# Low halves of twelve weight tiles through ScalarE and an adding DMA, S5 halves moved by ScalarE, and a new order: a one-core Hymba layer on Trainium2

## Chip, core and metric

One NeuronCore of one Trainium2 chip runs the whole layer. The metric is the device time of one execution in microseconds (us); lower is better. The names of the engines are those of the profile: PE (TensorE matmul), PEld (its weight load), DVE (VectorE), ACT (ScalarE), POOL (GpSimd), SP (SyncE, which here only issues DMAs).

## What is computed

Everything is float32, for 1024 positions and a model width of 1024. Cut to what matters here:

```python
z   = (LN of x) @ w_in        # split into S5 input 512 | S5 gate 512 | q-latent 256 |
                              # kv-latent 128 | rotary key 64 | MLA gate 512
# S5: bu = b @ u ; h[t] = a * h[t-1] + k * bu[t]  (complex, 32 groups x 64 states)
#     y = Re(c h) + d u ; gelu ; * sigmoid(y @ w_glu + b_glu) ; * silu(S5 gate)
# MLA: 4 heads, low-rank q and kv, shared rotary key, causal softmax over 128-query blocks
s  = einsum(q, k) * scale ; p = softmax(where(causal, s, -inf)) ; o = p @ v   # * silu(MLA gate)
u  = alpha * x + concat(S5, MLA) @ w_out
out = LayerNorm(u + sigmoid(u @ w_g) * (p_emb @ w_p))
```

## The kernel before

TensorE multiplies in the type fp32r, which holds fewer bits than float32. So every operand is split in two by `split(hi, lo, src)`: hi is a cast of src to fp32r, lo = src - hi. A product is three matmuls (`mm3`: hi*hi, lo*hi, hi*lo). In the profile hi and lo are two tiles, for instance `wh` and `wl` for a tile of the input weights (128 x 1024 elements, loaded as `wr`), or `wth` and `wtl` for the weights of the latents (128 x 896, loaded as `wtr`). The cast runs on ACT or DVE, the subtraction on DVE or POOL.

The input projection is cut into twelve weight tiles m (`w_load(m)`, `w_split(m)`): m = 0 to 3 give the S5 input (`xs`), 4 to 7 the S5 gate (`gs`), 8 to 11 the MLA gate (`gm`). Each tile makes two results `z` (512 columns of positions) of 24 matmuls each: eight slices of the contraction times three products. Four more tiles (`wt_split(k)`) make the latents (`lat`, result `zl`).

The S5 branch works on four blocks b of eight channel groups: `mats` builds the blocks' matrices on DVE (products of powers and parameters in `mo` and `mt`, split into `bbh` and `bbl` for the input side, `vvh` and `vvl` for the output side; TensorE transposes and multiplies them into `wt`, from which `wth`, `wtl`, `kt` come); `usplit` splits the input (`suu`); `state` multiplies (`w`, two halves q, each the sum of an even and an odd part of a PSUM tile), rotates (`rt`), scans over positions and puts the result into `hh`, then splits it into `hu`; `out` multiplies again (`y`). Half of the partitions of the S5 tiles hold real parts and half imaginary parts, and for the scan they have to change places: in `state`, a half-partition `add` of 64 x 256 writes from partitions 64..127 to 0..63 and the reverse (`re`, `im`), and half-partition subtractions and additions of 64 x 508 do it again for `hh`.

Attention (`scores`, `probs_t`, `pv`, `uv_out`) follows for 16 pairs of head and query-block pair (list `ATTEND`). DVE adds the mask and takes the row maximum `mx` in one instruction, a second one multiplies `mx` by -SCALE, and ACT takes the exponential. Then come `glu`, the output projection (`op`), the gate (`g`) and the final norm.

What sets the order: no instruction is issued where it is written. All are recorded (so all have one line in the profile, that of the recording helper: L449 before, L456 after), and `Plan.issue` places them by a list scheduler with a cost for each instruction and a priority. The priority is the place in the program, which for the side streams is set by lists of numbers (`MAIN`, `S5`, `LAT`, `GLU`, with `SHIFT`, `AHEAD`, `S5_LATE`). The planner also picks DVE or POOL for the operations that may go to either (`VG`); `NOT_G` lists tiles whose operations may not go to POOL. The result is a fixed order for each engine, and semaphores do the rest. Tiles of 128 x 1024 come from a pool of 40 buffers.

Of the kernel before, what the change touches and what calls it, by code (L numbers as in the profile page):

```python
# [34 lines left out]
P = 128  # L35
# [4 lines left out]
G = 32  # L40
# [12 lines left out]
def _cw_parts(c, bits, n):  # L53
# [11 lines left out]
PI_LO = float(np.nextafter(np.float32(math.pi), np.float32(0)))  # L65

MAIN = [
    ("w_load", 11), ("w_split", 9), ("w_load", 10), ("gm", 0, 0), ("w_split", 11), ("gm", 0, 1), ("gm", 1, 0),
    ("w_split", 10), ("wt_load",), ("gm", 1, 1), ("gm", 2, 0), ("wt_split", 1), ("gm", 2, 1), ("wt_split", 3),
    ("wt_split", 0), ("gm", 3, 0), ("gm", 3, 1), ("wt_split", 2), ("lat", 2), ("lat", 0), ("lat", 3), ("lat", 4),  # L70
    ("w_load", 4), ("w_load", 7), ("w_split", 4), ("w_load", 5), ("lat", 5), ("lat", 6), ("lat", 1), ("w_split", 5),
    ("lat", 7), ("w_load", 6), ("gs", 1, 0), ("gs", 0, 0), ("w_split", 7), ("w_split", 6), ("gs", 1, 1), ("gs", 0, 1),
    ("gs", 2, 0), ("gs", 2, 1), ("gs", 3, 0), ("gs", 3, 1),
]


S5 = [
    (0, "in", 0), (0, "mats", 0), (0, "mats", 0), (0, "usplit", 0), (0, "mats", 1), (0, "state", 0), (1, "mats", 1),
    (1, "in", 1), (2, "out", 0), (3, "mats", 1), (4, "mats", 0), (5, "usplit", 1), (6, "in", 2), (6, "mats", 2),
    (7, "state", 1), (7, "out", 1), (7, "mats", 2), (10, "mats", 2), (11, "phase", 1), (11, "usplit", 2),  # L80
    (11, "in", 3), (11, "state", 2), (13, "mats", 3), (14, "out", 2), (16, "mats", 3), (21, "mats", 3),
    (23, "usplit", 3), (26, "state", 3), (30, "out", 3),
]
# [25 lines left out]
class _Engine:
# [12 lines left out]
class Plan:  # L122
# [122 lines left out]
    @staticmethod  # L245
    def cost(eng, method, out, ins, kw):
        n = 1
        for d in out.shape[1:]:
            n *= d
        for a in ins:  # L250
            m = 1
            for d in a.shape[1:]:
                m *= d
            n = max(n, m) if method in ("bn_stats", "tensor_reduce", "activation") else n
        k = n / 1000.0
        ptr = sum(0.06 for x in ("scalar", "scalar1", "scalar2") if hasattr(kw.get(x), "ap"))
# [20 lines left out]
        if eng == "G":  # L277
            if kw.get("op") == ALU.pow:
                return 0.35 + 210 * k
            if method == "memset":  # L280
                return 0.03 + 0.88 * k
            return 0.25 + 0.82 * k if method == "tensor_scalar" else 0.16 + 2.14 * k
        return 0.06

    @staticmethod
    def shares(eng, method, out, ins):

        if eng == "G":
            return bool(ins)
# [26 lines left out]
    def issue(self):  # L316
# [69 lines left out]
        while len(order) < n:  # L386
# [66 lines left out]
def trunk(ctx, tc, I, out):  # L453
# [472 lines left out]
    def scores(h, qb):  # L926
# [723 lines left out]
```

## Time and profile before

| | before |
|---|---|
| median of 3 runs (lowest to highest) | 581.96 us (581.68 to 582.23) |
| the profiled execution: its own time, its span | 582.14 us, 580.4 us |
| TensorE clock granted, mean | 0.989 of full speed |
| busy: PE / PEld | 558.5 us (96%) / 475.5 us (82%) |
| busy: DVE / ACT / POOL | 455.3 us (78%) / 275.8 us (48%) / 90.1 us (16%) |
| moved by DMA | 76.67 MB, mean 132 GB/s |

The span is what the profiler sees of the program; 1.74 us of the profiled execution's time lies around it. Matmuls are pipelined: a matmul of 512 columns is shown with 0.39 us, but the next one starts about 0.23 us later, so "PE busy" says that matmuls follow each other, and the spacing of their starts says at what rate. The program has these stages: LayerNorm, transposes and the first projections (to about 56 us), the rest of the input projections with S5 beside it (to about 265 us), attention with the rest of S5 and the GLU (to about 398 us), output projection and gate (to 572 us), and a tail.

### The profile page before, as it was taken

To read this page: it belongs to the slowest core of one execution; us is meant where nothing else is said; L and a number is where in the kernel's file an instruction comes from. 1 tells how busy PE (TensorE), PEld (TensorE's weight loads), DVE (VectorE), ACT (ScalarE), POOL (GpSimd) and SP (SyncE) were. 2 spreads that over 40 slices of the span, in tenths; PEclk is the share of its full clock that TensorE was granted. 3 is DMA by queue.
4 is the path that set the end of the run, shared out by engine and by line. 5 is a ranking of instruction groups with operands and counts; after the bars stand their busy time and mean duration, and the time that the engine had idled before them with its cause. 6 is when DMAs were issued, how large, how long until landed. Compare 5 with 4: busy or idle time off the path is not lost.

```text
span 580.4 us, 8272 instructions
## 1 busy us (share of the span) xinstructions
PE 558.5 (96%) x2934; PEld 475.5 (82%) x2934; DVE 455.3 (78%) x973; ACT 275.8 (48%) x516; POOL 90.1 (16%) x100
## 2 busy tenths in 40 slices
PE   8998979999999999999999999999999999999994
PEld 5776868778888988888889999888888888888884
DVE  5989998899999988875998989876345337577666
ACT  6776324627176555445767887765111114123221
POOL 0100000302111153421622222202000001000000
PEclk9999989999999999999999999999999999999997
DMA  7897541533105222200113232509553567934301
GB/s 281 318 353 260 175 144 53 178 100 119 67 2 187 72 67 102 73 38 37 37 37 110 73 109 78 178 0 362 128 127 78 107 155 252 335 109 164 109 37 72
DMA packets 71865, 76.67 MB, mean 132 GB/s; under 512 B 37952, under 2 KB 52992, under 8 KB 71824
## 3 DMA queue, kind: packets, MB, share of 16 engines
q1 hardware_dynamic: 71824, 76.14, 40.3%
q8 instruction: 23, 0.38, 0.3%
q14 instruction: 18, 0.15, 0.1%
HBM read 50.47 MB, written 25.66 MB: 131 GB/s over the span
## 4 chain that ended last, share of the span: by engine, by line
PE 72%; DVE 18%; ACT 3%; DMA 3%; issue 2%; SPq 1%; POOL 0%; DVEq 0%; POOLq 0%
PE g L449 15%; PE op L449 15%; PE z L449 12%; PE s L449 6%; PE o L449 5%; PE zl L449 4%; PE glu L449 4%; PE y L449 2%; PE pt L449 2%; PE qn L449 2%; DVE bn L449 2%; DMA d_pp<-ppo 1%; DVE rt L449 1%; PE uv L449 1%; DVE p L449 1%
## 5 line engine op out<-in xcount | busy, mean ns | idle before, releaser
L449 PE MATMUL z<-xh,wh 128*128 128x512 f32 x192 | 76.4, 398 | 1.0 <-DVE xt L449 1.0
L449 PE MATMUL z<-xl,wh 128*128 128x512 f32 x192 | 76.5, 398 | 0.0
L449 PE MATMUL z<-xh,wl 128*128 128x512 f32 x192 | 76.0, 398 | 0.0
L449 PE MATMUL g<-wpl,uh 128*128 128x512 f32 (+1 forms) x136 | 51.2, 377 | 0.0
L449 PE MATMUL g<-wph,ul 128*128 128x512 f32 (+1 forms) x136 | 51.2, 376 | 0.0
L449 PE MATMUL g<-wph,uh 128*128 128x512 f32 (+1 forms) x136 | 51.2, 376 | 0.0
L449 PEld LDWEIGHTS z<-xh,wh 128*128 128x128 f32 x192 | 36.6, 191 | 8.5 <-DVE xt L449 1.2
L449 PEld LDWEIGHTS z<-xh,wl 128*128 128x128 f32 x192 | 36.7, 191 | 7.2 <-DVE wl L449 0.5
L449 PEld LDWEIGHTS z<-xl,wh 128*128 128x128 f32 x192 | 36.7, 191 | 6.8
L449 DVE SCALAR_TENSOR_TENSOR xr<-xr,op 128x512 f32<-128x512 f32 x16 | 11.0, 686 | 37.8 <-PE op L449 37.8
L449 ACT CAST uh<-xr 128x512 fp32r<-128x512 f32 x16 | 9.9, 621 | 62.3 <-DVE xr L449 49.0
L449 PEld LDWEIGHTS g<-wph,uh 128*128 128x128 f32 x136 | 25.6, 188 | 4.8
L449 PEld LDWEIGHTS g<-wpl,uh 128*128 128x128 f32 x136 | 25.6, 188 | 4.8
L449 PEld LDWEIGHTS g<-wph,ul 128*128 128x128 f32 x136 | 25.6, 188 | 4.6
L449 DVE CUSTOM_DVE_ANT_0 p<-s,mask 128x128 f32<-128x128 f32 (+7 forms) x32 | 23.7, 750 | 4.7 <-PE s L449 4.6
L449 ACT ACTIVATE sgg<-g 128x512 f32<-128x512 f32 (+1 forms) x17 | 9.6, 565 | 36.9 <-PE g L449 36.9
L449 DVE TENSOR_TENSOR ptl<-pt,pth 128x512 fp32r<-128x512 f32 (+3 forms) x48 | 25.6, 552 | 1.4 <-ACT pth L449 0.7
L449 ACT ACTIVATE p<-p,mx 128x128 f32<-128x128 f32 (+7 forms) x32 | 24.6, 771 | 3.6 <-DVE mx L449 3.4
L449 POOL TENSOR_TENSOR yml<-ymt,ymh 128x256 fp32r<-128x256 f32 x16 | 16.6, 1041 | 62.8 <-ACT ymh L449 56.7
L449 PE MATMUL op<-ysh,woh 128*128 128x512 f32 x64 | 24.9, 389 | 0.0
L449 PE MATMUL op<-ysh,wol 128*128 128x512 f32 x64 | 24.9, 389 | 0.0
L449 PE MATMUL op<-ysl,woh 128*128 128x512 f32 x64 | 24.9, 389 | 0.0
(372 smaller groups left out, 1642.4 us busy)
## 6 DMA issues: line engine op xcount, KB each, us to landing
wr<-in_w_fm SPq DMA_DIRECT2D x12, 512.0 KB, 6.1
x<-in_x SPq DMA_DIRECT2D x8, 512.0 KB, 8.9
d_pp<-ppo SPq DMA_DIRECT2D x8, 512.0 KB, 5.9
d_xln<-xt SPq DMA_DIRECT2D x16, 256.0 KB, 6.3
wor<-in_w_out SPq DMA_DIRECT2D x8, 512.0 KB, 5.1
xr<-d_xln SPq DMA_DIRECT2D x8, 512.0 KB, 6.1
d_ut<-ut SPq DMA_DIRECT2D x64, 64.0 KB, 1.9
utok<-d_ut SPq DMA_DIRECT2D x16, 256.0 KB, 4.5
```

Source lines behind the costliest of these rows:

```text
L449: getattr(self.real[ran[i]], method)(*ops[i]["args"], **kw)
```

## The change

It has four parts.

1. Twelve of the sixteen splits of the projection weights (m = 4 to 11, and the four latent tiles) get a new way, `split_dma`: hi is a cast on ACT, lo is written by ACT as -hi, and then a DMA that POOL issues reads the weights from DRAM a second time and adds them onto lo in place.
2. In the softmax the DVE instruction multiplies the masked score by -SCALE itself and takes the minimum, and the exponential takes -1 for its scale. The separate multiplication of `mx` (32 instructions) is gone.
3. In `state`, the sum of the two PSUM parts is one full DVE addition of 128 x 512 and four ACT copies move the halves; for `hh`, two full DVE operations and four ACT copies take the place of four half-partition DVE operations.
4. All lists of the order are new, `S5_LATE` goes from 50 to 260, and `NOT_G` has 19 names instead of 6.

```diff
+    def split_dma(hi, lo, src, dram):
+        cpy(A, hi, src)
+        act(lo, f(hi), AF.Copy, scale=-1.0)
+        Gp.dma_start(out=lo, in_=dram, accum_op=ALU.add)
...
+BY_DMA = range(4, 12)
-        split(h, l, r)                                  # w_split(m)
+        if m in BY_DMA:
+            split_dma(h, l, r, I["w_fm"][m])
+        else:
+            split(h, l, r)
...
-        split(h, l, wt[k])                              # wt_split(k)
+        split_dma(h, l, wt[k], I["w_tm"][k])
...
-            out=so, in0=si, in1=mk, scale=1.0, scalar=3.0 * MASK, op0=ALU.add, op1=ALU.max, accum_out=mx,
+            out=so, in0=si, in1=mk, scale=-SCALE, scalar=-3.0 * MASK, op0=ALU.add, op1=ALU.min, accum_out=mx,
-        V.tensor_scalar_mul(mx, mx, -SCALE)
-        act(p[:, :n], p[:, :n], AF.Exp, scale=SCALE, bias=mx, accum=sm)
+        act(p[:, :n], p[:, :n], AF.Exp, scale=-1.0, bias=mx, accum=sm)
...
             cpy(A, t, ps[:, :, 1])                      # s5_state, for each q
+            add(t, ps[:, :, 0], t)
             for par in range(2):
                 for c, dst in enumerate((re, im)):
-                    src = slice(64 * c, 64 * c + 64)
-                    add(dst[64 * par : 64 * par + 64, 2 * q : 2 * q + 2], ps[src, par::2, 0], t[src, par::2])
+                    cpy(A, dst[64 * par : 64 * par + 64, 2 * q : 2 * q + 2], t[64 * c : 64 * c + 64, par::2])
...
-        n1 = NCH - 1
+        sub(x1, x1, x2)
+        add(x3, x3, x4)
         for par in range(2):
-            r = slice(64 * par, 64 * par + 64)
-            sub(hh[0:64, par::2, 1:], x1[r, :, :n1], x2[r, :, :n1])
-            add(hh[64:P, par::2, 1:], x3[r, :, :n1], x4[r, :, :n1])
+            for c, x in enumerate((x1, x3)):
+                cpy(A, hh[64 * c : 64 * c + 64, par::2, 1:], x[64 * par : 64 * par + 64, :, : NCH - 1])
...
-S5_LATE = 50
-NOT_G = ["bbl", "kd", "mo", "pl", "uql", "vvl"]
+S5_LATE = 260
+NOT_G = ["bbl", "kb", "kd", "p", "ppo", "ppr", "qd", "re", "suu", "tl", "uql", "vvl", "wol", "wpl", "wqrl", "wtl",
+         "wuvl", "xl", "yTl"]
-SHIFT = [(S5, -3920), (LAT, -1380), (GLU, -1400)]
+SHIFT = [(S5, -2680), (LAT, -630), (GLU, -1890)]
```

Counted by engine, with a row for each instruction in the program, DVE has 32 `mx`, 7 `wl` and 2 `wtl` fewer, takes back from POOL the eight `qd`, the eleven scalings of `p` and seven of `kb`, and exchanges 32 half-partition operations of `re` and `im` for 8 full ones, 16 of `hh` for 8. ACT has 8 `wl`, 4 `wtl`, 16 `hh`, 16 `re` and 16 `im` more, and 13 table loads instead of 11. POOL has 12 DMAs. The matmuls are the same.

Where the order moves, at three places.

DVE, before, at the first block of S5 matrices (b = 0). The numbers behind names count tiles in the order of the program; `mo_318` is block 0's input matrix, `mo_351` block 0's output matrix, `ph`, `ec` and `es` are the S5 phases:

```order
L449 TENSOR_TENSOR ph_311<-ec_309,w2c_300 128x8x16
L449 TENSOR_TENSOR ph_312<-es_310,w2s_301 128x8x16
L449 TENSOR_TENSOR mo_318<-pr_248,X_273 128x1024
L449 TENSOR_TENSOR ec_309<-ph_311,ph_312 128x8x16
L449 TENSOR_TENSOR mt_319<-pi_249,Y_274 128x1024
L449 TENSOR_TENSOR ph_311<-ec_309,w2s_301 128x8x16
L449 TENSOR_TENSOR ph_312<-es_310,w2c_300 128x8x16
L449 TENSOR_TENSOR ph_313<-ec_309,w2c_303 128x8x32
L449 TENSOR_TENSOR es_310<-ph_311,ph_312 128x8x16
L449 TENSOR_TENSOR mo_318<-mo_318,mt_319 128x1024
```

And now, where `mo_347` is the input matrix of block 1 and `mo_352` the output matrix of block 0:

```order
L456 TENSOR_TENSOR mo_347<-pr_248,X_273 128x1024
L456 TENSOR_TENSOR mt_348<-pi_249,Y_274 128x1024
L456 TENSOR_TENSOR w2c_306<-w2c_306,w2t_308 128x16
L456 TENSOR_TENSOR mo_347<-mo_347,mt_348 128x1024
L456 TENSOR_TENSOR ph_311<-ec_309,w2c_300 128x8x16
L456 TENSOR_TENSOR ph_312<-es_310,w2s_301 128x8x16
L456 TENSOR_TENSOR mo_318<-pr_248,X_273 128x1024
L456 TENSOR_TENSOR ec_309<-ph_311,ph_312 128x8x16
L456 TENSOR_TENSOR mt_319<-pi_249,Y_274 128x1024
L456 TENSOR_TENSOR bbl_350<-mo_347,bbh_349 128x1024
L456 TENSOR_TENSOR mo_352<-pr_248,CX_277 128x1024
L456 TENSOR_TENSOR mt_353<-pi_249,CY_278 128x1024
```

The addition `mo_318<-mo_318,mt_319` follows six rows later, behind that of `mo_352`. Block 0's input matrix now comes behind those of block 1's input and most of block 0's output. PE, before, at the first use of that matrix (`wt<-ic,bbh`), inside the tile `z_327`, the last of the S5 input:

```order
L449 MATMUL z_327<-xh_150,wh_217 128x512
L449 MATMUL z_327<-xl_151,wh_217 128x512
L449 MATMUL z_327<-xh_150,wl_218 128x512
L449 MATMUL z_327<-xh_154,wh_217 128x512
L449 MATMUL wt_346<-ic_280,bbh_320 128x160 x3
L449 MATMUL wt_347<-ic_280,bbh_320 128x160 x3
```

And now, inside `z_337`, the first tile of the MLA gate, whose weights are the first of the new kind:

```order
L456 MATMUL z_337<-xh_170,wh_325 128x512
L456 MATMUL z_337<-xl_171,wh_325 128x512
L456 MATMUL wt_342<-ic_280,bbh_320 128x160 x3
L456 MATMUL wt_343<-ic_280,bbh_320 128x160 x3
L456 MATMUL z_337<-xh_170,wl_326 128x512
```

The use stands behind four matmuls of `z_327` before, behind all 24 of it and 17 of `z_337` now: 37 matmuls of 512 columns later. ACT, now, at the second weight tile of the new kind (`wh_367` is its hi, `wl_368` its lo):

```order
L456 CAST wh_367<-wr_323 128x1024
L456 COPY kt_341<-wt_344 128x64
L456 CAST wtl_340<-wt_344 128x256
L456 COPY kt_341<-wt_344 128x64
L456 COPY ic_280<-cxh_279 128x8x32
L456 ACTIVATE wl_368<-wh_367 128x1024
```

Between the cast and the negative copy stand four small instructions; in the order before, neither the copy nor a DMA stands there, and DVE subtracts. POOL, now, with the DMAs that add the weights onto lo:

```order
L456 DMA wl_326<-in_w_fm 128x1024
L456 DMA wl_368<-in_w_fm 128x1024
L456 MEMSET zk_335 112x512
L456 DMA wl_371<-in_w_fm 128x1024
L456 TENSOR_TENSOR kt_362<-kt_362,kb_366 128x8x16
```

And PE, now, where that lo is used for the first time:

```order
L456 MATMUL z_395<-xh_150,wh_367 128x512
L456 MATMUL z_395<-xl_151,wh_367 128x512
L456 MATMUL z_395<-xh_150,wl_368 128x512
L456 MATMUL z_395<-xh_154,wh_367 128x512
L456 MATMUL w_381<-suu_359,wth_339 128x256
```

Two matmuls of that tile stand ahead of the one that reads the new lo, and the POOL queue holds the second DMA, a memset and the third DMA ahead of a product for the S5 kernel (`kt`). The second half of the `w` matmuls of `state` for block 0 stands two rows behind it.

More of the change, by code (lines that the diff above doesn't have):

```diff
@@ L67 @@
 MAIN = [
[L68 to L72, printed above, removed]
+    ("w_load", 11), ("gm", 0, 0), ("w_split", 9), ("w_load", 10), ("w_split", 10), ("wt_load",), ("gm", 0, 1),
+    ("w_split", 11), ("gm", 1, 0), ("gm", 2, 0), ("gm", 2, 1), ("wt_split", 0), ("wt_split", 1), ("wt_split", 2),
+    ("gm", 1, 1), ("wt_split", 3), ("lat", 0), ("gm", 3, 0), ("w_load", 4), ("gm", 3, 1), ("lat", 6), ("w_load", 5),
+    ("lat", 4), ("lat", 7), ("lat", 2), ("w_load", 6), ("w_split", 5), ("lat", 5), ("w_split", 6), ("gs", 1, 0),
+    ("lat", 3), ("w_load", 7), ("w_split", 4), ("gs", 0, 0), ("gs", 1, 1), ("lat", 1), ("gs", 0, 1), ("w_split", 7),
     ("gs", 2, 0), ("gs", 2, 1), ("gs", 3, 0), ("gs", 3, 1),
@@ L77 @@
 S5 = [
[L78 to L82, printed above, removed]
+    (0, "mats", 0), (0, "in", 0), (0, "mats", 1), (0, "mats", 0), (0, "usplit", 0), (0, "mats", 1), (1, "state", 0),
@@ L83 @@
+    (3, "mats", 0), (3, "in", 1), (4, "mats", 1), (4, "usplit", 1), (6, "out", 0), (6, "mats", 2), (8, "in", 2),
+    (8, "state", 1), (8, "out", 1), (9, "mats", 2), (10, "mats", 2), (11, "usplit", 2), (12, "phase", 1),
+    (13, "state", 2), (13, "out", 2), (14, "in", 3), (14, "mats", 3), (20, "mats", 3), (23, "mats", 3),
+    (25, "usplit", 3), (26, "state", 3), (30, "out", 3),
 ]
 LAT = [
-    (16, "lat_alloc"), (17, "lat_norm", 1), (17, "lat_transpose", 1), (17, "lat_norm", 0), (19, "fold"),
@@ L86 @@
-    (20, "lat_transpose", 0), (20, "q_rope", 1), (20, "q_rope", 0), (21, "mask"), (23, "q_nope", 0, 0),
-    (23, "q_rope_t", 0), (23, "q_rope_t", 1), (24, "q_nope", 0, 1), (27, "q_nope", 1, 0), (27, "q_nope", 2, 0),
-    (27, "q_nope", 1, 1), (27, "q_nope", 2, 1), (27, "q_nope", 3, 0), (27, "q_nope", 3, 1),
+    (10, "lat_alloc"), (17, "lat_norm", 1), (19, "lat_norm", 0), (20, "mask"), (20, "lat_transpose", 1), (20, "fold"),
+    (20, "lat_transpose", 0), (20, "q_rope", 0), (22, "q_nope", 2, 0), (22, "q_rope", 1), (23, "q_rope_t", 0),
@@ L89 @@
+    (23, "q_nope", 0, 0), (23, "q_nope", 0, 1), (24, "q_rope_t", 1), (27, "q_nope", 1, 0), (27, "q_nope", 1, 1),
+    (30, "q_nope", 2, 1), (30, "q_nope", 3, 0), (30, "q_nope", 3, 1),
 ]
 GLU = [
-    (30, "glu_y", 2), (31, "glu_w"), (33, "glu_y", 0), (34, "glu_gs", 1), (35, "glu_gs", 2), (36, "glu_y", 1),
-    (37, "glu_yg", 2), (38, "glu_yg", 1), (38, "glu_gs", 3), (39, "glu_y", 3), (39, "glu", 1, 0), (39, "wo_load", 1),
-    (39, "glu_gs", 0), (39, "glu_yg", 0), (39, "glu", 0, 0), (39, "glu", 0, 1), (39, "glu_yg", 3), (39, "glu", 2, 0),
@@ L94 @@
-    (39, "glu", 3, 0), (39, "glu", 2, 1), (39, "glu", 1, 1), (41, "glu", 3, 1), (41, "wo_load", 0),
-    (42, "wo_split", 0),
+    (30, "glu_y", 0), (31, "glu_y", 2), (32, "glu_w"), (34, "glu_gs", 2), (36, "glu_y", 1), (37, "glu_gs", 1),
+    (37, "glu_gs", 3), (38, "glu_yg", 1), (39, "wo_load", 0), (39, "glu_y", 3), (39, "glu_yg", 3), (40, "glu_yg", 2),
+    (40, "wo_load", 1), (40, "glu_gs", 0), (40, "glu", 1, 0), (40, "glu_yg", 0), (40, "glu", 0, 0), (40, "glu", 0, 1),
+    (40, "glu", 2, 0), (40, "wo_split", 0), (41, "glu", 3, 0), (42, "glu", 1, 1), (42, "glu", 2, 1),
@@ L96 @@
+    (42, "glu", 3, 1),
 ]
@@ L98 @@
 ATTEND = [
-    (0, 0), (0, 3), (0, 1), (0, 2), (1, 0), (1, 3), (2, 0), (2, 1), (1, 1), (2, 2), (1, 2), (2, 3), (3, 0), (3, 2),
-    (3, 1), (3, 3),
-]
-S5_LATE = 50
-NOT_G = ["bbl", "kd", "mo", "pl", "uql", "vvl"]
-AHEAD = {"fold": 700, "glu": -1400, "glu_gs": 690, "glu_w": 670, "glu_y": -30, "glu_yg": -410, "in": 160, "lat_alloc": -440, "lat_norm": -890, "lat_transpose": -1800, "mask": -470, "mats": 200, "out": 300, "phase": -830, "q_nope": -1100, "q_rope": 600, "q_rope_t": 510, "state": -370, "usplit": -100, "wo_load": -560, "wo_split": 620}
-SHIFT = [(S5, -3920), (LAT, -1380), (GLU, -1400)]
+    (0, 0), (0, 3), (0, 1), (0, 2), (1, 0), (1, 3), (2, 0), (2, 1), (1, 1), (2, 2), (2, 3), (1, 2), (3, 0), (3, 3),
+    (3, 2), (3, 1),
+]
+BY_DMA = range(4, 12)
+S5_LATE = 260
+NOT_G = ["bbl", "kb", "kd", "p", "ppo", "ppr", "qd", "re", "suu", "tl", "uql", "vvl", "wol", "wpl", "wqrl", "wtl", "wuvl", "xl", "yTl"]
+AHEAD = {"fold": 200, "glu": -960, "glu_gs": -310, "glu_w": -60, "glu_y": -70, "glu_yg": -370, "in": 300, "lat_alloc": -100, "lat_norm": 40, "lat_transpose": -700, "mask": -470, "mats": -40, "out": -70, "phase": -600, "q_nope": -140, "q_rope": 300, "q_rope_t": -300, "state": -500, "usplit": 460, "wo_load": 130, "wo_split": -730}
+SHIFT = [(S5, -2680), (LAT, -630), (GLU, -1890)]
 class _Engine:
@@ L277, in cost @@
         if eng == "G":
+            if method == "dma_start":
+                return 1.2
             if kw.get("op") == ALU.pow:
@@ L288, in shares @@
         if eng == "G":
-            return bool(ins)
+            return bool(ins) and method != "dma_start"
         if eng != "V":
@@ L432, in issue @@
                 end = dma + 0.9
+            if e == "G" and o["bytes"]:
+                dma = max(dma, end) + o["bytes"] / 179e3
+                end = dma + 1.2
             done[i] = end
```

## Prediction

> **What bounds the kernel now.** I read the page first: busy time of the engines, and the slices.
>
> ```profile
> span 580.4 us, 8272 instructions
> PE 558.5 (96%) x2934; PEld 475.5 (82%) x2934; DVE 455.3 (78%) x973; ACT 275.8 (48%) x516; POOL 90.1 (16%) x100
> PE   8998979999999999999999999999999999999994
> ```
>
> PE is the bound, and its matmuls are untouched, so the change can win only where PE idles or runs slowly, and lose wherever PE comes to wait. The table by stage says where that is (columns: stretch, its length, then busy time of PE, PEld, DVE, ACT, POOL, granted clock, DMA share, GB/s).
>
> ```profile
> 0.00:56.00 56.00, 48.58 (x229) 38.27 (x230) 46.52 (x117) 37.13 (x58) 3.39 (x13) 1.00 0.83 302
> 56.00:80.00 24.00, 24.00 (x107) 19.87 (x107) 23.93 (x118) 7.55 (x14) 0.00 (x0) 1.00 0.58 194
> 80.00:92.00 12.00, 9.07 (x31) 7.19 (x30) 11.01 (x18) 3.82 (x7) 0.59 (x2) 0.72 0.20 56
> 92.00:135.00 43.00, 41.52 (x215) 34.38 (x214) 39.01 (x64) 19.56 (x43) 7.88 (x7) 1.00 0.40 125
> 135.00:265.00 130.00, 129.24 (x713) 112.04 (x712) 115.03 (x208) 69.14 (x143) 33.17 (x31) 1.00 0.22 77
> 265.00:398.00 133.00, 131.78 (x856) 118.55 (x855) 113.65 (x281) 95.49 (x190) 34.40 (x35) 1.00 0.26 86
> 398.00:572.00 174.00, 174.00 (x793) 145.06 (x792) 101.81 (x162) 42.71 (x61) 9.78 (x11) 1.00 0.52 156
> 572.00:580.40 8.40, 0.34 (x3) 0.13 (x2) 4.31 (x9) 0.38 (x1) 0.90 (x1) 0.65 0.17 62
> ```
>
> From 398 us PE has no gap at full clock, so the time is set by when the output projection starts. Ahead of it PE idles 7.4 us in the first stage (LayerNorm, not changed), 2.9 at 80 to 92, 1.5 at 92 to 135, and 0.8 + 1.2 = 2.0 from 135 to 398. The waits of PE and the chain give the names.
>
> ```profile
> PE xt L449 <- DVE xt L449: 4.2, 3, 1.9
> PE wt L449 <- ACT bbh L449: 2.9, 1, 2.9
> PE wt L449 <- DVE im L449: 1.0, 1, 1.0
> PE y L449 <- DVE im L449: 0.6, 2, 0.3
> ```
> ```profile
> 78.17 1.14 DVE mo L449
> ...
> 79.51 1.14 DVE mt L449
> ...
> 81.58 1.15 DVE mo L449
> ...
> 82.75 1.05 ACT bbh L449
> ```
> ```profile
> 80.31 0.39 PE L449 MATMUL z<-xh,wl 128*128 128x512 f32 x1
> 80.53 0.39 PE L449 MATMUL z<-xh,wh 128*128 128x512 f32 x1
> 83.85 1.57 PE L449 MATMUL wt<-ic,bbh 128*128 128x160 f32 x6 [2.93 <-ACT bbh L449]
> ...
> 85.73 0.63 PE L449 MATMUL z<-xh,wl 128*128 128x512 f32 x1
> 86.15 0.63 PE L449 MATMUL z<-xh,wh 128*128 128x512 f32 x1
> ...
> 89.95 0.40 PE L449 MATMUL z<-xh,wh 128*128 128x512 f32 x1
> 90.18 0.40 PE L449 MATMUL z<-xl,wh 128*128 128x512 f32 x1
> ```
> ```profile
> 85.22:89.95 4.73, 4.73 (x13) 3.71 (x12) 4.73 (x9) 1.89 (x5) 0.01 (x1) 0.51 0.39 111
> ```
>
> The matmuls start 0.22 to 0.23 us apart at 80.3 and at 90, 0.42 us apart at 86, where the clock is granted at 0.51. So the wait costs 3.1 us (83.85 - 80.53 - 0.23) and its aftermath 11 matmuls times 0.2 = 2.2 us, together with small change 5.5. In the first stage the longest wait is 1.9 us and the clock stays at 1.00. In the stretch of 56 to 80 us DVE is busy for 23.93 of 24 us, so what is taken from it there, ahead of `mo`, moves the whole chain up.
>
> **The change part by part.** Prices:
>
> ```profile
> 60.24 1.22 DVE L449 TENSOR_TENSOR wl<-wr,wh 128x1024 fp32r<-128x1024 f32 x1
> L449 DVE TENSOR_TENSOR wl<-wr,wh 128x1024 fp32r<-128x1024 f32 x11 | 13.3, 1218 | 1.0 <-DMA d_pp<-ppo 0.9
> L449 ACT CAST wh<-wr 128x1024 fp32r<-128x1024 f32 x12 | 12.5, 1051 | 2.0 <-DMA wr<-in_w_fm 2.0
> L449 DVE TENSOR_TENSOR hh<-rt,rt 64x508 f32<-64x508 f32 x16 | 10.9, 680 | 0.3
> L449 DVE TENSOR_TENSOR im<-w,wt 64x256 f32<-64x256 f32 x16 | 6.8, 427 | 0.3
> L449 DVE TENSOR_TENSOR rt<-rt,rt 128x512 f32<-128x512 f32 x3 | 2.0, 683 | 0.0
> L449 DVE TENSOR_SCALAR mx<-mx 128x1 f32<-128x1 f32 x32 | 4.6, 149 | 0.2
> DMA to landing us min/median/max: 3.2/6.1/8.1
> 93.42 0.48 ACT L449 CAST wtl<-wt 128x384 fp32r<-128x384 f32 x1
> ...
> 96.10 0.44 ACT L449 CAST ic<-cxh 128x256 fp32r<-128x256 f32 x1
> L449 POOL TENSOR_TENSOR wl<-wr,wh 128x1024 fp32r<-128x1024 f32 x1 | 3.3, 3321 | 16.5 <-ACT wh L449 16.5
> L449 POOL TENSOR_TENSOR kb<-kt 128x128 f32<-128x128 f32 x7 | 4.3, 610 | 26.4 <-ACT kt L449 26.1
> L449 POOL TENSOR_TENSOR tl<-tr,th 128x1024 fp32r<-128x1024 f32 x1 | 2.4, 2384 | 11.3 <-ACT th L449 11.3
> ```
>
> *S5 halves.* `hh`: 16 half operations (10.9 us) become 8 full ones of 0.683 (5.5), so DVE saves 5.4; `re` and `im`, priced alike, are 32 x 0.427 = 13.7 us and become 8 of 0.683, saving 8.2. ACT gains 48 copies, at most 0.6 each: up to 29 us. DVE is relieved, but a block's chain gets two hops to ACT and does not become shorter itself: between `w` and `hu` stand DVE's four `hh` = 2.7 us before, two full ones and four copies now, some 1.4 + 2 us. ACT has the room (19.56 of 43 us busy at 92 to 135), so I cost this at nothing; if ACT is behind there, the price is the wait for `y`, one copy row (0.6) per block, 2.4 in all.
>
> *The lo by DMA.* DVE loses seven `wl` of 1.218 us (8.5) and two `wtl`; ACT gains twelve copies of about 1.05 us, the nearest row being the cast. What lies on the path is the `wl` at 60.24, whose going pulls the DVE chain ahead of `mo` up by 1.13 us (next start 61.37). In exchange, lo now comes one DMA after ACT's copy. No row shows an adding DMA or one issued by POOL. Bounds from plain DMAs of the same 512 KB: 3.2 us at the least, 8.1 at the most. The adding DMA also reads its destination; I take 5.5, an estimate: the smallest landing, 3.2, plus a second pass over 512 KB at the first stage's 302 GB/s, 1.7, plus 0.6 for the issue, as much as POOL's small `kb` takes. It lies nearer the median than the least.
>
> What room has it? After `bbh` (90.9 us, below) ACT has, up to the end of the second copy (`wl_368`), 13 small instructions, ten of which took 3.1 us (93.42 to 96.54) before, and two of 1.05: end at 97.0. PE has from there 35 matmuls of 512 columns, 32 of 160 (six took 1.37 us at the halved clock, so 0.11 each) and 8 of 256 (0.12, by length): 12.4 us, so it reads `wl_368` at 103.3. Room 6.3. I walked the others the same way: `wl_326` has over 20 us; `wl_371`, `wl_394`, the four `wtl` and `wl_507`, `wl_532`, `wl_544` have 5.9 to 7.6; the last has more. So at 5.5 nothing waits on paper; I allow 0.7 us for one that misses. At 3.2 it is nothing, at 8.1 eight rooms of 6.3 to 7 are missed by 1 to 2 us each (rival B). Queues: each DMA stands in POOL's order and waits there for ACT's copy. Behind the third waits the product `kt` of block 1, at most one copy, 1.05 us, late, on the way to `y<-suu,tl`, whose wait was 0.3. SP's queue is not lengthened; 5.9 MB more are read, and the DMA share is 0.40 and 0.22 where they fall.
>
> The Trainium skill, "DMA: Bandwidth & Descriptors", section on the anatomy of a DMA on the SWDGE (gpsimd) path, puts one at about 2.0 us and bytes over 436e3: 3.2 us for these 512 KB, an estimate for a plain one. By it no room is missed and the sum below would be 576.4. No run here shows such a DMA yet.
>
> *The order.* DVE now builds block 1's input matrix (three large operations) and block 0's output matrix (three) and one `bbl` ahead of the last addition of `mo_318`. From where `mo_318` started, 78.09, less 1.13 and less the two small `ph` that now follow (0.4), `mo_347` starts at 76.5; then ten large operations at the spacing of 1.14 and eight small ones of 0.2 on average: 13.0, so `mo_318` is complete at 89.5. ACT has its queue ahead (`vvh`, `xs`, `suu`) and ends `bbh` near 90.9. PE comes to it 37 matmuls later than before: 80.53 + 37 x 0.2266 = 88.9, plus the last one's 0.23. It waits 2.0 us instead of 3.1, and since 1.9 us left the clock at 1.00 in the first stage, the 2.2 us of slow matmuls go. **Gain 5.5 - 2.0 = 3.5.** What is late next is again `bbh`, behind DVE.
>
> At 92 to 135 PE waited 1.0 for `wt<-im` and 0.9 in smaller pieces on DVE, which now loses its `wl`, `wtl` and half of the S5 halves there; by the same walk PE meets `hu` of block 0 0.7 us early. **Gain 1.9 - 0.7 = 1.2.**
>
> *Softmax.* The 32 `mx` (4.6 us of DVE) lie in each row block's way to the exponential, but PE is hardly short there: of the 2.0 us of gaps from 135 to 398 I take half, **1.0**. They return to DVE, against this, 26 operations of POOL (scalings of `p`, `qd`, `kb`); DVE was 88% busy at 135 to 265 and the sum of all parts leaves it lighter.
>
> Sum: -3.5 - 1.2 - 1.0 + 0.7 = -5.0. The profiled execution took 582.14 us with the span, 0.18 above the median of 581.96: 577.1, so 577.0 against the median.
>
> **The rivals.** *B, the adding DMA lands late; slower.* Five tight places (`wl_368`, `wl_371`, `wl_394`, and two of the S5 gate) each wait for what the latency has beyond about 6.4 us, and PE has nothing else, since its order is fixed. At 8.5 us that is 10.5, and with the other terms (-5.7) 587. It decides from 6.4 + 5.7 / 5 = 7.5 us on. For it: the median of plain ones is 6.1 with the same size, and POOL took 3.3 us for `wl` against 2.4 for `tl` of the same shape, so it can be held up beside a busy DVE. Against it: at 92 to 265 us the DMA share is low, and the 6.1 come from stretches where several loads queue. The Trainium skill, "SBUF — State Buffer", section "Who interferes with whom", says that a DVE copy, cast or tensor_scalar in a 2-port mode locks the port pair shared with GpSimd, DMA descriptor generation included; the two rows would bear it out with 0.94 us per DMA, which alone does not reach 7.5.
>
> *C, the wait only moves.* If `bbh` ends 1.2 us later than I walked, PE waits over 3.1 us at 89, and the clock halves again: 5.5 there as before, and about half a `wl` of the rest is eaten: 582.14 - 1.2 - 1.0 + 0.7 + 1 = about 581.6, no change. For it: ACT's queue ahead of `bbh` is longer than before. Against it: the tenth `mo` would have to slip by a whole large operation.
>
> *D, all DVE waits go.* The 37 matmuls cover the chain wholly, because DVE gains on it elsewhere too, the gaps at 92 to 398 vanish: -5.5 - 1.5 - 2.0 - small change 0.5 = 572.6. For it: DVE loses some 27 us of work (8.5 + 13.6 + 4.6). Against it: it is full to 92 us, and only 1.13 of the 27 lie there.
>
> **How the numbers follow.** Forecast A, 577.0 (its own range 574.5 to 580.4): 0.50. D: 0.16. C: 0.10. B: 0.24. Changes under 0.2% (1.2 us), about what a measurement can tell, count as none. Faster is A and D, 0.66; same C, 0.10; slower B, 0.24. The range goes from 571.0 under D to 586.0, which takes in C and the weaker half of B; above lie latencies of over 8.2.
>
> **What would show it.** A wait of about 2 us at `wt<-ic,bbh` near 89 us with a clock of 1.00 behind it, and none of over 0.7 for a `z` or `zl` on a DMA: A. A DMA from ACT's copy to landing of over 7.5 us, and PE waits at `z` named for `wl`: B. A clock near 0.5 at 90 us: C. No wait of over 0.5 at `bbh`: D. The prediction is wrong altogether if the output projection starts earlier or later for another reason, such as S5 or the GLU arriving late at the end of attention, where the new lists move whole steps that I only walked by their loads.

## The result and the profile after

| | before | changed |
|---|---|---|
| median of 9 runs each on one chip (lowest to highest) | 581.86 us (580.42 to 583.70) | 583.52 us (581.69 to 585.71) |
| ratio to before, 95% interval | 1 | 1.0053 (1.0035 to 1.0071) |
| the profiled execution: its own time, span, clock | 582.14 us, 580.4 us, 0.989 | 584.54 us, 582.8 us, 0.991 |

The change makes the kernel about half a percent slower. Single executions of 790 to 3150 us, one each in e1, e5, e10 and e13 below, are left out of the ratios. The forecast was 577.0: the measured time lies inside the range, on the wrong side of the kernel before. The page and the table by stage of the changed kernel (columns as above):

```profile
span 582.8 us, 8275 instructions
PE 559.0 (96%) x2934; PEld 477.4 (82%) x2934; DVE 436.4 (75%) x936; ACT 309.5 (53%) x575; POOL 64.0 (11%) x76
q0 software_dynamic: 1728, 6.03, 5.9%
```
```profile
80.00:92.00 12.00, 9.41 (x42) 7.52 (x41) 12.00 (x17) 4.53 (x6) 0.00 (x0) 0.97 0.25 75
92.00:135.00 43.00, 41.30 (x206) 35.12 (x206) 33.04 (x67) 28.45 (x59) 3.69 (x6) 0.93 0.60 165
135.00:265.00 130.00, 127.71 (x697) 111.24 (x696) 97.67 (x195) 87.03 (x170) 25.02 (x23) 1.00 0.41 108
265.00:398.00 133.00, 130.03 (x858) 117.78 (x857) 114.22 (x256) 101.03 (x207) 23.66 (x22) 1.00 0.26 87
```

The work moved as counted: DVE 19 us lighter, ACT 34 us heavier, POOL lighter, and 6.03 MB go through a new queue, that of the DMAs that POOL issues. In this profile the relief of DVE does not show as less idle time of TensorE behind the first stage. At 80 to 135 us TensorE idles 2.6 + 1.7 = 4.3 us (4.4 before) and again runs at a reduced clock, only later (0.93 at 92 to 135). From 135 to 398 it idles 2.3 + 3.0 = 5.3 us where it idled 2.0. (In the first stage it idled 6.1 us here and 7.4 before.) The output projection starts at 400.1 instead of 397.4 us, and from there both kernels are alike. TensorE's waits, then the place of the halved clock, then DVE and ACT ahead of it:

```profile
PE wt L456 <- ACT bbh L456: 2.6, 1, 2.6
PE z L456 <- DMA wl<-in_w_fm: 2.0, 2, 1.7
PE o L456 <- DVE ptl L456: 1.1, 2, 0.9
PE zl L456 <- DMA wtl<-in_w_tm: 0.8, 1, 0.8
PE s L456 <- ACT qnh L456: 0.8, 1, 0.8
```
```profile
88.64 0.39 PE L456 MATMUL z<-xl,wh 128*128 128x512 f32 x1
91.61 1.57 PE L456 MATMUL wt<-ic,bbh 128*128 128x160 f32 x6 [2.59 <-ACT bbh L456]
93.49 0.63 PE L456 MATMUL z<-xh,wh 128*128 128x512 f32 x1
```
```profile
77.25 1.22 DVE L456 TENSOR_TENSOR mo<-pr,X 128x1024 f32<-128x1024 f32 x1
...
89.14 1.22 DVE L456 TENSOR_TENSOR mo<-mo,mt 128x1024 f32<-128x1024 f32 x1
90.51 1.04 ACT L456 CAST bbh<-mo 128x1024 fp32r<-128x1024 f32 x1
```

PE came to `bbh` at 88.9 us, as walked; `mo` was complete at 90.4 (walked 89.5) and `bbh` at 91.55 (walked 90.9). The wait is 2.7 us instead of 2.0, and the matmuls behind it have 0.63 us each again, until 98. The adding DMAs, from issue to landing, and ACT's copy and POOL's issue for them:

```profile
DMA to landing us min/median/max: 5.2/6.8/10.1
```
```profile
L456 ACT ACTIVATE wl<-wh 128x1024 fp32r<-128x1024 f32 x8 | 8.6, 1076 | 0.1
L456 POOL DMA_DIRECT2D wl<-in_w_fm x8 | 7.4, 925 | 119.4 <-PE wt L456 41.6 <-PE z L456 28.6 <-ACT wl L456 24.3
```

### The profile page after: what moved, and what is told of

It is laid out like the page before. It is cut to its first block, busy times and chain, and to the rows that moved or that the text cites. A ratio compares the mean times of both kernels' runs of the same rounds, so it can differ in the third digit from the quotient of the medians.

```text
span 582.8 us, 8275 instructions
## 1 busy us (share of the span) xinstructions
PE 559.0 (96%) x2934; PEld 477.4 (82%) x2934; DVE 436.4 (75%) x936; ACT 309.5 (53%) x575; POOL 64.0 (11%) x76
## 3 DMA queue, kind: packets, MB, share of 16 engines
q0 software_dynamic: 1728, 6.03, 5.9%
## 4 chain that ended last, share of the span: by engine, by line
PE 71%; DMA 9%; issue 9%; DVE 6%; ACT 4%; POOL 1%; SPq 1%; DVEq 0%; POOLq 0%
PE g L456 15%; PE op L456 15%; PE z L456 13%; PE s L456 6%; PE o L456 5%; PE glu L456 4%; DMA x<-in_x 3%; DMA wl<-in_w_fm 3%; PE zl L456 2%; PE qn L456 2%; PE pt L456 2%; PE y L456 2%; DMA bc<-in_c_x 1%; DMA wtl<-in_w_tm 1%; PE wt L456 1%
## 5 line engine op out<-in xcount | busy, mean ns | idle before, releaser
L456 POOL TENSOR_TENSOR rstd<-ve,half 128x1 f32<-128x1 f32 (+1 forms) x10 | 7.2, 721 | 191.0 <-DVE ve L456 181.6
```

Source lines behind the costliest of these rows:

```text
L456: getattr(self.real[ran[i]], method)(*ops[i]["args"], **kw)
```

## The experiments

"Order kept" means that the planner's order of every engine is that of the named kernel, and only the instructions told of are left out, put in or replaced at their places. All ratios are to the kernel before, run on the same chip in between; the changed kernel stands at 1.0053.

**The halved clock (e1, e4).**

```diff
+    # ahead of the first wt<-ic,bbh, n = 11 (changed kernel) or 12 (before)
+    for _ in range(n): tensor.matmul(wt_psum[:, 1, :], z_weights, z_moving, start=True, stop=True)
```

> The changed kernel with its order kept on every engine; ahead of the first wt<-ic,bbh TensorE gets 11 idle-time matmuls of 512 columns (2.5 us at full clock) on data that is there already, into the part of the PSUM tile that is overwritten afterwards. They add to the matmuls and change no result. In the changed kernel's profile TensorE stands 2.7 us there and then runs eight matmuls at half clock, about 1.9 us lost. Theory 1 (the halved clock after the wait is one of the places where the forecast gain went): the clock stays at 1.00 and the kernel is 1.7 to 2.2 us faster than the changed kernel, about 581.4 against its median of 583.5. Rival (the time comes back further on): the next wait, for wl<-in_w_fm at 113 to 115 us, ends when the DMA lands, not when TensorE comes, so the gain is eaten there: the clock is at 1.00, that wait grows from 1.7 to over 3 us, and the kernel is at most 0.6 us faster.

> The kernel before with its order kept and 12 such idle-time matmuls (2.7 us) ahead of the first wt<-ic,bbh, in a wait of 3.1 us. Theory 1: the clock stays at 1.00, the 11 matmuls at half clock (2.2 us) go, and the kernel is 1.5 to 2.2 us faster than before, about 580. Rival (DVE sets the pace after it): the wait for wt<-im at 110 us grows from 1.0 us by what is gained, and the kernel is at most 0.6 us faster.

Measured: e4 0.9975 (0.9962 to 0.9989), e1 1.0033 (1.0012 to 1.0054). In the kernel before the theory holds; the matmuls fill the wait and the clock stays:

```profile
79.88 2.88 PE L457 MATMUL wt<-xh,wh 128*128 128x512 f32 x12
82.95 0.90 PE L464 MATMUL wt<-ic,bbh 128*128 128x160 f32 x6 [0.18 <-ACT bbh L464]
```
```profile
80.00:92.00 12.00, 11.81 (x63) 9.70 (x62) 12.00 (x20) 6.87 (x17) 0.59 (x2) 1.00 0.32 91
```

In the changed kernel neither theory holds: `bbh` came later in that execution, 1.3 us of wait were left, and the clock fell a little behind it, at 94 us, for 6.8 us:

```profile
87.96 2.65 PE L464 MATMUL wt<-xl,wh 128*128 128x512 f32 x11
91.93 0.90 PE L471 MATMUL wt<-ic,bbh 128*128 128x160 f32 x6 [1.31 <-ACT bbh L471]
94.03 1.54 PE L471 MATMUL wt<-ic,bbl 128*128 128x160 f32 x6 [0.23 <-DVE bbl L471]
95.88 0.63 PE L471 MATMUL z<-xl,wh 128*128 128x512 f32 x1
```

Its interval overlaps that of the changed kernel, so no gain is shown. But that execution had the lowest clock of the eleven counted, 0.990. Two others reached 0.997, the clock of e4's profile, and took 580.6 and 581.9 us. So with the filling matmuls the clock seems to have stayed in some executions and fallen in others, which no profile shows.

**The adding DMA (e2, e6, e7, e9).** e2 leaves the twelve DMAs out; e6 sends four loads later; e7 gives the kernel before all twelve; e9 gives it one.

```diff
-        Gp.dma_start(out=lo, in_=dram, accum_op=ALU.add)       # e2: lo stays -hi
...
-    SP: wtr wtr wtr wtr ... tr                                 # e6
+    SP: ... tr wtr wtr wtr wtr
...
-        sub(lo, src, f(hi))                                    # e7: m = 4..11 and wt; e9: m = 8 only
+        act(lo, f(hi), AF.Copy, scale=-1.0); Gp.dma_start(out=lo, in_=dram, accum_op=ALU.add)
```

> The changed kernel with its order kept, without the twelve adding DMAs; lo is then only -hi, so this part of the product is left out and only the time counts. Theory 2 (the adding DMAs land too late): the waits of TensorE named for wl and wtl (2.0 + 0.8 us, with the restart 3.3) go and the kernel is 2.8 to 3.5 us faster than the changed one, about 580.4. Rival (what follows was waiting anyway, S5 chain or ACT): the waits take another name and the kernel is at most 1 us faster.

Measured: 0.9991 (0.9973 to 1.0009), 0.62% or 3.6 us faster than the changed kernel. Theory 2 holds, at its upper end. The mean granted clock of e2's runs is that of the changed kernel's, 0.992, so the clock does not explain the gain. The stage from 92 to 135 us of e2 has 0.3 us of idle time left, and the wait for `bbh` ahead of it is shorter too: 91.08 - 88.97 - 0.23 = 1.9 us instead of 2.7, with the clock at 1.00 behind it:

```profile
92.00:135.00 43.00, 42.66 (x220) 35.51 (x220) 35.47 (x69) 32.84 (x65) 1.04 (x3) 1.00 0.43 140
```
```profile
76.72 1.22 DVE L471 TENSOR_TENSOR mo<-pr,X 128x1024 f32<-128x1024 f32 x1
...
88.97 0.39 PE L471 MATMUL z<-xl,wh 128*128 128x512 f32 x1
91.08 0.90 PE L471 MATMUL wt<-ic,bbh 128*128 128x160 f32 x6 [1.72 <-ACT bbh L471]
```

> The changed kernel with its order kept but for the four loads wtr on SP's queue (448 KB each, issued from 102.8 to 106.1 us), which now go out after tr<-d_k, at about 116 us; they are first read at about 136. The third adding DMA took 10.2 us from issue to landing beside these loads, the others alone 5.0 to 5.5. Theory 2a (an adding DMA shares the engines with the loads in flight and is late for that reason): it lands in 5 to 6 us, TensorE's wait of 1.7 us for it at 115 goes, and the kernel is 1 to 1.9 us faster than the changed one. Rival (an adding DMA is erratic by itself): it still takes over 8 us, and the time stays within 0.5 us.

Measured: 1.0032 (1.0015 to 1.0050), 0.2% or 1.2 us less than the changed kernel, though the intervals overlap. The third DMA landed in 5.7 us instead of 10.1, and the waits named for `wl` and `wtl` went from 2.8 to 0.3 us. So the lateness of that one came from the loads beside it (the wait, and the third DMA alone, of e6):

```profile
PE z L484 <- DMA wl<-in_w_fm: 0.3, 1, 0.3
```
```profile
wl<-in_w_fm POOLq DMA_DIRECT2D x1, 512.0 KB, 5.7
```

> The kernel before with its order kept; only the twelve lo are made in the new way (ACT's negative copy and the adding DMA at the place where DVE or POOL subtracted). Theory 2 (the landing of 5 to 10 us is more than this program has between lo and its first use): TensorE waits for wl and wtl in most of the twelve places, some 2 us each where the next tile follows directly, and the kernel is 5 to 15 us slower than before, although the wl at 60 us no longer stands ahead of mo. Rival (what DVE gains pays for it): within 1.5 us of before.

Measured: 1.0667 (1.0646 to 1.0688), 39 us slower, far over what theory 2 gave: a wait reaches 7 us, and the clock falls behind most of them, to a mean of 0.965.

```profile
PE z L464 <- DMA wl<-in_w_fm: 22.1, 4, 6.9
PE zl L464 <- DMA wtl<-in_w_tm: 7.4, 2, 4.9
```

> The kernel before with its order kept; one single lo, that of the weight tile m = 8 which DVE subtracts at 60.2 us and PE first reads at about 84, is made by ACT's negative copy and the adding DMA. In the two kernels with all twelve this one landed at 66.7 to 67.6 us. Theory 5 (the new way pays where its latency is covered and DVE is full): nothing waits for it, the DVE chain ahead of bbh comes 1.1 us earlier, the wait of 2.9 us for bbh falls to about 1.8, and the kernel is 1 to 3 us faster than before (the upper end where the halved clock goes too). Rival (the chain is held by something else, or the DMA disturbs the loads beside it): the wait stays over 2.5 us and the time within 0.5 us.

Measured: 1.0013 (0.9996 to 1.0030): the rival. The DMA was ready in time and nothing waited for it. But with the `wl` gone, DVE met three waits, and the wait for `bbh` did not shrink:

```profile
61.55 0.19 DVE L464 TENSOR_TENSOR pr<-mg,ecs 128x32 f32<-128x32 f32 x1 [0.43 <-ACT ecs L464]
63.46 0.23 DVE L464 TENSOR_TENSOR pw<-pi,pr 128x64 f32<-128x64 f32 x1 [0.37 <-DMA d_xln<-xt]
68.54 0.49 DVE L464 TENSOR_SCALAR CX<-bc,ng 128x512 f32<-128x512 f32 x1 [0.82 <-DMA bc<-in_c_x]
```
```profile
PE wt L464 <- ACT bbh L464: 3.4, 1, 3.4
```

The first two, 0.80 us, the `wl` had covered. The third, 0.82 us, came with the adding DMA. The load `bc<-in_c_x` went out 1.0 us behind it (62.2 and 61.2 us) and took 6.3 us to land, where it takes 3.3 us in the kernel before and is there at 64.9, 2.8 us ahead of its reader. Before, e9, and e10 below, where DVE waits 2.5 us for it:

```profile
bc<-in_c_x SPq DMA_DIRECT2D x1, 256.0 KB, 3.3
bc<-in_c_x SPq DMA_DIRECT2D x1, 256.0 KB, 6.3
bc<-in_c_x SPq DMA_DIRECT2D x1, 256.0 KB, 8.1
```

So half of the rival is the DMA disturbing the loads beside it. The changed order shows the same. From DVE's `mg<-pe_q,pe_b` near 60 us to the first `mo` pass 16.2 us in e2 and e3, which have no adding DMA, 17.1 in the changed kernel, and 16.4 to 18.3 in the other six runs that have its DMAs (e1, e5, e6, e13, e14, e16).

**DVE's subtraction in the changed order (e3, e12).** In e3 it takes the place of ACT's copy; in e12 the planner orders anew.

```diff
-        act(lo, f(hi), AF.Copy, scale=-1.0); Gp.dma_start(out=lo, in_=dram, accum_op=ALU.add)
+        sub(lo, src, f(hi))
```

> The changed kernel with its order kept, but at the place of ACT's negative copy stands DVE's subtraction of 1.1 to 1.2 us, as before, and the DMA is gone: twelve instructions move back from ACT and POOL to DVE, 14 us of DVE work. Theory 2: since DVE has room from 92 us on in the changed order (33.0 of 43 us busy, then 97.7 of 130), this is as fast as the kernel without the adding DMAs, within 1 us, so 2 to 3.5 us faster than the changed one. Rival (DVE needs the relief): the S5 chain or the DVE-fed waits slip by the 1.2 us each and the kernel is no faster than the changed one.

> The changed kernel with its lists, its fused maximum and its S5 halves, but with the old split for all sixteen weight tiles, ordered anew by the planner under the new lists (so the order differs from the changed kernel's). It tells what the adding DMA is worth in an order that knows of it against one that knows of the subtraction. Theory 2 (the DMA costs more than it relieves): within 2 us of before, so faster than the changed kernel. Rival (the new lists live from the relief of DVE): 3 us or more slower than before.

Measured: e3 1.0235 (1.0208 to 1.0261), e12 1.0369 (1.0351 to 1.0387). The rival in both, and more. In e3, in-order DVE stands 6.5 us at one subtraction, though its cast had ended 5.4 us earlier (what it waited for the profile does not name), and the S5 block behind it is late (first two rows). In e12 one subtraction comes over 12 us behind its cast, since S5 work stands ahead of it on DVE (the other two):

```profile
195.47 1.23 DVE L549 TENSOR_TENSOR wl<-wr,wh 128x1024 fp32r<-128x1024 f32 x1 [6.46 <-issue]
PE y L471 <- DVE hu L471: 7.1, 2, 6.5
```
```profile
PE z L456 <- DVE wl L456: 10.7, 1, 10.7
PE pt L456 <- DVE ptl L456: 8.1, 1, 8.1
```

So the new lists only work with the new code: e7 puts the new split into the old order and loses 39 us, e12 plans the old split under the new lists and loses 21. (The new split planned anew under the old lists was not run.)

**Softmax and S5 halves (e8, e11, e14).** e8 has both in the order of before, e11 the fused maximum alone; e14 undoes the halves in the changed order.

```diff
-    add(dst[64*par:64*par+64, 2*q:2*q+2], ps[src, par::2, 0], t[src, par::2])    # DVE, e8; e14 the reverse
+    add(t, ps[:, :, 0], t)                                                       # DVE, once
+    copy(dst[64*par:64*par+64, 2*q:2*q+2], t[src, par::2])                       # ACT, four times
```

> The kernel before with its order kept, with the fused negative maximum (32 small DVE instructions gone) and the S5 halves moved by ACT (DVE 32 + 16 half operations become 8 + 8, ACT 48 copies more), no adding DMA. Theory 4 (these two relieve DVE where TensorE hardly waits for it): TensorE's waits named for DVE im and mx (1.0 + 0.6 + 0.3 us) shrink, 0.5 to 1.5 us faster than before. Rival (each half now goes over ACT and comes later): y and wt wait longer, 0.5 to 2 us slower.

> The kernel before with its order kept and only the fused negative maximum (32 DVE instructions of 0.15 us gone). With the S5 halves on ACT beside it the ratio was 1.0040. Theory 4a (ACT's copies cost that): this one is at or below before, 0 to 1 us faster. Rival (the fused form itself delays something): it is slower than before by 1 us or more.

> The changed kernel with its order kept, but the S5 halves are done as before: at the places of ACT's 48 copies stand DVE's half-partition additions and subtractions (0.42 to 0.68 us each), and the full DVE operations are gone; 13.6 us back to DVE, 48 instructions off ACT. Theory 4 (the hop over ACT costs more than DVE gains, as in the order before, where the two edits cost 0.40% and the fused maximum alone gained 0.1%): 0.5 to 2 us faster than the changed kernel. Rival (the changed order is made for the copies, DVE is full without them): 1 us or more slower than the changed kernel.

Measured: e8 1.0040 (1.0023 to 1.0058), e11 0.9991 (0.9975 to 1.0008), e14 1.0198 (1.0173 to 1.0223). In the order before, the halves on ACT cost some 0.5% (1.0040 against 0.9991): the rival of theory 4. From 135 to 398 us TensorE idles 5.3 us in e8 and 1.7 in e11. Rows of e8: `hu` is late, and three S5 copies stand in ACT's queue ahead of attention's casts and the next scaling of `p`, for which TensorE waits 1.8 us.

```profile
PE y L464 <- DVE hu L464: 2.2, 2, 1.1
PE pt L464 <- ACT p L464: 1.8, 1, 1.8
```
```profile
277.51 0.39 ACT L1228 COPY re<-wt 64x256 f32<-64x256 f32 x1
277.91 0.41 ACT L1228 COPY im<-wt 64x256 f32<-64x256 f32 x1
278.33 0.41 ACT L1228 COPY re<-wt 64x256 f32<-64x256 f32 x1
278.76 0.59 ACT L464 CAST pth<-pt 128x512 fp32r<-128x512 f32 x1
...
280.30 1.15 ACT L464 ACTIVATE p<-p,rrec 128x1024 f32<-128x1024 f32 x1
```

In the changed order the sign is the reverse: without the copies the kernel is 1.4% slower than with them, `y` waits 6.1 us for `im`. The same edit is worth -0.5% or +1.4%, by the order that it stands in.

**The loss from 135 to 398 us (e5, e13, e16).** e5 moves one product `gsr` 26 instructions later on DVE; e13 gives ACT's scalings of `p` to POOL; e16 has the lists `GLU` and `ATTEND` of before.

> The changed kernel with its order kept but for one instruction: on DVE the second product gsr<-gsr,yT (2.04 us at 359.5 us), which stands ahead of two row maxima of attention, comes 26 instructions later, into an idle place of 1.5 us at 372. Theory 3 (the new lists made a wait near the end of attention): TensorE's waits for ptl at 363.8, 365.7 and 369.5 (0.9 + 0.6 + 0.2, with the restart 2.2 us more than in a stretch without waits) go, and the kernel is 1.7 to 2.2 us faster than the changed one: 1.002 to 1.0025 of before, where the changed one stood at 1.0053. Rival (something else is late there, ACT's casts or the scalings of p that no longer run on POOL): the waits stay under another name and the gain is under 0.6 us.

> The changed kernel with its order kept; the 22 scalings of p that ACT does there are given to POOL, which is idle at those times (before, POOL did eleven of all). Theory 3b (ACT, with its new copies and these scalings, makes TensorE wait from 290 to 370 us): the waits at 291.7 (0.8 us), 363.8 (0.9) and 365.7 (0.6) shrink, 1 to 2.5 us faster than the changed kernel, ratio 1.001 to 1.0035. Rival (POOL is slower at it, 0.5 to 1.0 us each plus a hop, and the scaling is on the way from the exponential to the transposes): no faster, or 1 to 4 us slower.

> The changed kernel with the lists GLU and ATTEND of before (and the numbers of SHIFT and AHEAD that belong to them), planned anew; TensorE's order is the same up to the middle of attention. Theory 3c (the new order of the GLU leaves TensorE without filler between the last steps of attention): the losses from 340 to 380 us go from about 4.6 us above a stretch without waits to 2 or less, and the kernel is 1 to 2.5 us faster than the changed one, ratio 1.001 to 1.0035. Rival (attention's chain is slower in the changed kernel whatever the GLU does): the waits stay, within 0.7 us of the changed kernel.

Measured: 1.0052 (1.0038 to 1.0065), 1.0071 (1.0051 to 1.0091), 1.0054 (1.0034 to 1.0075). None is faster than the changed kernel; the rivals hold. e16 does take away the waits at 360 us and idles 1.9 us from 265 to 398 us instead of 3.0, which is 1.1 us in the profile; the intervals are too wide for the times to show or exclude it:

```profile
265.00:398.00 133.00, 131.10 (x856) 118.00 (x855) 114.05 (x256) 101.22 (x206) 25.32 (x21) 1.00 0.25 83
```

Most of the loss is not the adding DMAs': e2, without them, still idles 4.7 of the 5.3 us from 135 to 398. What makes it up stays open.

**What the runs point to (e10, e15).** e10: the adding DMA for m = 8, the fused maximum and 8 filling matmuls; e15: the fused maximum and 12 filling matmuls, both in the order of before.

> The kernel before with its order kept, with three things: the adding DMA for m = 8 alone, the fused negative maximum, and 8 idle-time matmuls (1.8 us) in what remains of the wait for bbh. If the three add up: 1.1 us from the wait, about 1.5 us from the clock (the filled kernel was at 0.9975 of before), up to 0.5 from the maximum, so 2.5 to 3.5 us faster than before, ratio 0.994 to 0.996. Rival (what is gained at 84 us is lost at the next wait for DVE, at 105 to 110): no better than the filled kernel, 0.9975.

> The kernel before with its order kept, the fused negative maximum and 12 idle-time matmuls in the wait for bbh: the two edits that each came out at or below before (0.9991 and 0.9975). If they add up: 0.9960 to 0.9975, about 578.5 us where before is 580.5. Rival (the clock falls by chance of its phase elsewhere): no better than 0.998.

Measured: e10 0.9980 (0.9964 to 0.9997), the rival: its wait for `bbh` was 3.4 us behind the eight matmuls, since `bc<-in_c_x` was late behind the adding DMA. e15 0.9956 (0.9943 to 0.9969), median 578.07 us where before had 580.66 beside it: faster than both kernels by 2.5 us or more, with no weight tile changed.

## Why the prediction was wrong

The count of the work held: DVE became 18.9 us lighter and ACT 33.7 heavier. The terms that failed, in the order of the sum:

1. **"What lies on the path is the `wl` at 60.24, whose going pulls the DVE chain ahead of `mo` up by 1.13 us."** The row showed DVE busy without a gap, and I took the work behind it to be free to move up. e9 shows what was hidden: waits for ACT's `ecs` and a transfer, 0.80 us. And I priced what the adding DMA does to other transfers at nothing ("SP's queue is not lengthened; 5.9 MB more are read, and the DMA share is 0.40 and 0.22 where they fall"). But the first one falls at 58 us, where the share was 0.58, beside the loads `bc` that DVE reads next. In the changed kernel `mo` started 0.75 us later than walked and the wait was 2.7 us, not 2.0. In e2, without the DMAs, `mo` started at 76.7 (walked 76.5) and the wait was 1.9. So the walk of DVE was right within 0.2 us, and the DMAs upset it.

2. **"Since 1.9 us left the clock at 1.00 in the first stage, the 2.2 us of slow matmuls go."** One execution of one stage was no bound. At the same place, behind nearly the same wait, the clock stayed before and fell in e9, where the twelve small matmuls took 2.8 us instead of 1.5 (and the granted clock is 0.50 from 50.0 to 53.4 us):

```profile
50.00 1.53 PE L449 MATMUL xt<-ident,x 128*128 128x128 f32 x12 [1.90 <-DVE xt L449]
49.98 2.82 PE L464 MATMUL xt<-ident,x 128*128 128x128 f32 x12 [1.84 <-DVE xt L464]
```

It also fell behind a wait of 2.7 us in the changed kernel, behind 1.3 us and a run of small matmuls in e1, and not behind 1.9 us in e2. And it differs from run to run of the same kernel: over the 104 runs of the kernel before beside the experiments, the mean granted clock lay between 0.986 and 0.997, with 33 runs at 0.989 (mean 581.8 us) and 15 at 0.997 (579.1 us). The profiled execution on which I built had 0.989, near the slow end, so part of the gain was not there to be won in other executions. The size was also low, 2.2 us: before, the clock is 0.50 for 6.8 us, with 6.0 us of work in them, which costs 3.0.

```profile
83.05:89.88 6.83, 6.03 (x17) 5.06 (x18) 6.83 (x12) 3.52 (x7) 0.00 (x0) 0.50 0.28 79
```

The Trainium skill, "TensorE: Matmul & The Clock Gate", Part 1, says that the clock has two levels and is set by activity in a window of about 3.4 us that runs free of the program. The traces agree: the slow stretches here, 6.8 us before, in the changed kernel and in e1, are two such windows, that of e9's first stage, 3.4 us, is one, and the same wait ends with or without a slow stretch. Steps 1 and 2 together: 3.5 us forecast, 0.3 found in the profile (from 80 to 100 us TensorE idles 2.9 us before and 2.6 now, at a mean clock of 0.83 in both).

3. **"So at 5.5 nothing waits on paper; I allow 0.7 us."** The latency alone was sized well: 5.0 to 5.5 us where nothing else was under way. Beside loads it was 6.6 to 10.1. Adding DMAs that are issued close together also land late: the four `wtl`, issued 1.8 us apart, landed 2.7, 4.0 and 2.7 us apart, after 5.0, 5.8, 8.0 and 8.9 us (one load `wr` went out among them). I priced a lone DMA, and did not lay the SP queue beside POOL's: the loads `wtr` are issued from 102.8 us, the third adding DMA at 105.2. The DMAs cost 3.6 us (e2) instead of 0.7: 2.8 us are the waits named for `wl` and `wtl`, and the rest is about the 0.8 us by which the wait for `bbh` is longer (item 1). The Trainium skill, "DMA: Bandwidth & Descriptors", section on the SWDGE path, gives 3.2 us for a plain DMA of this size, an estimate; the adding ones of 512 KB took 5.2 at the least.

4. **"if ACT is behind there, the price is the wait for `y`, one copy row (0.6) per block, 2.4 in all"**, costed at nothing. In the old order the halves on ACT cost 0.5%, 2.8 us, the size of that bound; in the new one, made for them, they are needed (e14). The term's sign hangs on the order.

5. **Softmax, 1.0 us:** e11 gives 0.9991 (0.9975 to 1.0008), at most 1.5 us and not told from nothing. The 1.0 for the stage from 135 to 398 us did not come. The changed kernel idles 3.3 us more there, 2.7 of them also without the DMAs (e2). This is the largest part of the miss, and its cause stays open.

6. **The 1.2 us from 92 to 135 us** are in e2: its idle time is 0.3 us against 1.5. The late DMAs take them away again.

So rival C happened (the wait moved and the clock fell again), with a weaker B (the DMAs land late, 3.6 us rather than 10.5). I had given each a chance of its own and a time of its own, where they come together: 582.1 - 1.2 of the stage above, + 3.6 would already be slower than before.

## What to carry to other kernels

An engine that is busy without a gap hides what else its chain waits for; before a removed instruction is booked as a gain, ask for each of the next ones when its other inputs arrive. A transfer that takes work off an engine can make the loads beside it late (here 6.3 us instead of 3.3), so ask also who reads those. A list schedule and the code it was tuned for are one thing: here the new split in the old order loses 39 us and the new lists with the old split 21, so such an edit is judged in its own order, and an old order with a small edit (e15) may beat the new one. Where TensorE must wait, matmuls on data already there cost nothing here (e4, e15) and kept its clock where they filled the wait.

## What the runs showed of the hardware

- An adding DMA of 512 KB from DRAM onto SBUF takes POOL 0.88 us to issue (1.06 the first time) and 5.2 to 5.5 us to land when alone. Four of 448 KB, issued 1.8 us apart with one load among them, land 3.1 us apart on average, which is 148 GB/s.
- A load of 256 KB took 3.3 us from issue to landing in the kernel before, and 6.3 and 8.1 us in e9 and e10, where an adding DMA of 512 KB was issued 1.0 and 0.6 us ahead of it.
- Behind a wait of 1.9 us of TensorE the clock stayed in one execution, and behind 1.8 us at the same place it was halved for 3.4 us in another (before, e9). A mean granted clock that differs by 0.008 from run to run goes with 2.7 us in this kernel; a profile is one draw of it.
